# Attention's block rows as step sequences of their own, a third buffer for the high part of the split weights, one general temporary less

## The chip, the cores and the metric

One Trainium2 chip, one of its cores. The metric is the device time of one execution in microseconds (us); the median of several runs counts, and one more execution is profiled.

## The reference, cut to what matters

One layer: a normalized input, one projection into 57 column tiles of 128, three branches (RWKV-7 time mixing in six pairs of heads, causal pooling in four groups, stick-breaking attention in six pairs of heads), a gate on each, and an output projection. All in float32, 512 tokens of width 2048.

```python
h = _rms(x, norm_g[l])
proj = h @ w_in[l]
pa, pb, pc = _split(proj, (A_COLS, B_COLS, C_COLS))
...
y = jnp.concatenate([ya, yb, yc], axis=-1).astype(x.dtype) @ w_out[l]
x = x + y.astype(x.dtype)
```

The branch that the change rewrites is attention. Per block row of 128 queries:

```python
z = jnp.einsum('bhqd,bhkd->bhqk', q[:, :, q0:kend], k[:, :, :kend])
causal = jnp.arange(kend)[None, :] < (q0 + jnp.arange(SB_BLOCK))[:, None]
log_1m = jnp.where(causal, jax.nn.log_sigmoid(-z), 0.0)
after = lax.cumsum(log_1m, axis=3, reverse=True) - log_1m
w = jnp.where(causal, jnp.exp(jax.nn.log_sigmoid(z) + after), 0.0)
outs.append(jnp.einsum('bhqk,bhkd->bhqd', w, v[:, :, :kend]))
```

The cumulative sum over keys is what the kernel does with a scan on VectorE. RWKV's recurrence over tokens is done in eight chunks of 64 tokens, each a few matmuls that hand a state on to the next chunk.

## The kernel before

**The projection is the backbone.** Tiles are worked one after the other in the order of `tile_order`: for each pair p of heads q, k, v and gate of attention, then k, r of the next pair, v and gate of RWKV. A product in full precision is made of three matmuls in a reduced format (`three`): activations and weights are split into a high part and a low part, and high by high, low by high and high by low are summed (`hh`, `hl` for activations, `wh`, `wl` for weights). A column tile is 16 x 3 matmuls of 128x128 by 512 tokens, into a PSUM bank `pj` of which there are two.

**The weights come as a stream of halves**, 128x1024 each: 108 of the input projection and 32 of the output projection. For each, `split_weights` (L445) issues the load into `raw` on SyncE's queue (SP), casts it to `wh` on ScalarE and subtracts to `wl` on VectorE. `raw`, `wh` and `wl` have two buffers each. The next half is fetched when a half is begun, with a priority that puts it `AHEAD` = 300 in front of what the program has written so far.

**Everything else is side work**, written as Python generators (here: step sequences): `rwkv(p)`, `attention(p)`, `pooling(g)`. They advance in `pump`, called after every matmul of the projection. `Pace` keeps a model of when each engine is through with what, and a sequence yields a time: `need(...)` (tiles are ready and a PSUM bank is free, with a margin) or `soon(...)` (tiles ready, 1.5 us early allowed). `spawn` adds a sequence. The result is a fixed order on every engine; at run time each engine works its own list in order and waits by semaphores.

**Attention** makes the normalized q and k, splits them, and then does for each of the two heads three groups of block rows: widths 512, 512 (384 + 128) and 256. For each: matmuls into the bank `z`; ScalarE copies it to `w`; GpSimd masks the diagonal block (`affine_select`); ScalarE makes `n` (Abs, Exp, Ln) and `m` (Relu); one `soon(n, m)`; VectorE scans `n` and subtracts (`w<-w,n`); ScalarE takes the exponential (`w<-w`). The last three come out of one step. `n` has two buffers and `m` one. Then `w` is transposed (`wT`) and multiplied with v (`o`).

**RWKV** makes `bk`, `amr`, `bx` and the block inverses (`xblk`, `lt`), and at the end runs through the eight chunks: matmul `s`, then VectorE writes two pieces of `uv` (by `ec`), which the next chunk's `s` reads.

16 general temporaries of 128x528 (`TP`) are shared by all sequences. In the trace the ScalarE, VectorE and GpSimd work has the line L212 (a helper records it), matmuls L380, transposes L384, and DMAs L226.

Of the kernel before, what the change touches and what calls it, by code (L numbers as in the profile page):

```python
# [8 lines left out]
F32 = mybir.dt.float32  # L9
F32R = mybir.dt.float32r  # L10
AF = mybir.ActivationFunctionType
ALU = mybir.AluOpType

P = 128
# [43 lines left out]
DL = 4.0  # L58
QUICK = 1.8
SCAN = 150  # L60
TP = 16


def tile_order():
# [153 lines left out]
def hybrid_trunk_kernel(ctx: ExitStack, tc: tile.TileContext, x, xT, w_in, w_out, vecs, consts, up_w, pool_w, out):  # L218
    nc = tc.nc
# [20 lines left out]
    def name(s):  # L240
        uid[0] += 1
        return f"{s}_{uid[0]}"
# [6 lines left out]
    def tmp(s="t", cols=T):  # L249
        return tp.tile([P, TW], F32, tag="t", name=name(s))[:, 0:cols]  # L250
# [137 lines left out]
    def need(*tiles, tag=None, margin=MARGIN):  # L388
        def at():
            t = max([pace.ready.get(Pace.key(a), 0.0) for a in tiles] + [0.0])  # L390
            return margin + (max(t, pace.bank_at(tag, BANKS[tag])) if tag else t)

        return at
# [17 lines left out]
    def soon(*tiles):  # L411
        return need(*tiles, margin=-1.5)

    def spawn(gen):
        tasks.append([gen, lambda: 0.0])
# [27 lines left out]
    HK = KT // 2  # L443

    def split_weights(src):  # L445
        raw = wp.tile([P, HK * P], F32, tag="raw", bufs=2, name=name("raw"))
        dma(out=raw, in_=src)
        wh = wp.tile([P, HK * P], F32R, tag="wh", name=name("wh"))
        wl = wp.tile([P, HK * P], F32R, tag="wl", name=name("wl"))
        act.copy(out=wh, in_=raw)  # L450
        dve.tensor_tensor(wl, raw, wh.bitcast(F32), ALU.subtract)
        return wh, wl
# [101 lines left out]
    def rwkv(p):  # L554
# [8 lines left out]
        sq = tmp("sq")  # L563
# [54 lines left out]
        m1 = tmp("m1")  # L618
        bv = scratch(f"bv{p % 2}", "bv")
        dve.scalar_tensor_tensor(m1, rs, col(V_RK), kp, ALU.mult, ALU.mult)  # L620
        yield soon(rs)

# [171 lines left out]
        mu = gb("mu")  # L796
        block_sum(mu, bmean_r, yp2)
        dve.tensor_tensor(y, y, mu, ALU.subtract)
        sq = tmp("sq")
        act.activation(sq, y, AF.Square)  # L800
        sqp = split(sq)
# [2 lines left out]
        block_sum(var, bmean_r, sqp)  # L804
        act.activation(sq, var, AF.Ln, bias=eps_gn)
        act.activation(sq, sq, AF.Exp, scale=-0.5)
        dve.scalar_tensor_tensor(y, y, col(V_GNG), sq, ALU.mult, ALU.mult)
        dve.scalar_tensor_tensor(y, y, col(V_GNB), bv, ALU.add, ALU.add)
        gate = yt[Y_TILE[("a", p)]]
# [5 lines left out]
    def attention(p):  # L815
        while p > 0 and not done.get(("att", p - 1)):
            yield None
        qk = []
        for kind, gain, slot in (("cq", nvec[:, 12:13], "aq"), ("ck", vec[:, V_KN:V_KN + 1], "ak")):
            while (kind, p) not in got:  # L820
                yield None
            raw = got.pop((kind, p))
            dst = scratch(slot, kind)
            sq = tmp("qs")
            act.activation(sq, raw, AF.Square)
            sqp = split(sq)
            yield need(*sqp, tag="g")
            ms = gb("qm")
            block_sum(ms, bmean_r, sqp)
            y0, t = newton_rsqrt(ms, RMS_EPS, eps_rms, sq)  # L830
            dve.scalar_tensor_tensor(raw, raw, gain, y0, ALU.mult, ALU.mult)
            dve.tensor_tensor(dst, raw, t, ALU.mult)
            qk.append(dst)
        q, k = qk
        yield need(q, k)
        kr = tmpr("kr")
        act.copy(out=kr, in_=k)
        klo = tmpr("klo")
        dve.tensor_tensor(klo, k, kr.bitcast(F32), ALU.subtract)
        head = []  # L840
        for h in range(2):
            s = slice(h * HD, (h + 1) * HD)
            other = hi if h == 0 else lo
            q2 = ap.tile([P, T], F32R, tag="q2", name=name("q2"))
            k2 = ap.tile([P, T], F32R, tag="k2", name=name("k2"))
            act.copy(out=q2[s, :], in_=q[s, :])
            dve.tensor_tensor(q2[other, :], q[s, :], q2[s, :].bitcast(F32), ALU.subtract)
            act.copy(out=k2[s, :], in_=k[s, :])
            act.copy(out=k2[other, :], in_=k[s, :])
            kl2 = ap.tile([P, T], F32R, tag="kl2", name=name("kl2"))  # L850
            pool.tensor_copy(out=kl2[s, :], in_=klo[s, :])
            pool.tensor_copy(out=kl2[other, :], in_=klo[s, :])
            blocks = {}
            for segs, width in ((((3, 0),), 512), (((2, 0), (0, 384)), 512), (((1, 0),), 256)):
                yield need(q2, k2, kl2, tag="g")
                z = gb("z")
                for i, off in segs:
                    mm(z[:, off:off + (i + 1) * P], q2[:, i * P:(i + 1) * P], k2[:, 0:(i + 1) * P], True, False)
                    mm(z[:, off:off + (i + 1) * P], q2[:, i * P:(i + 1) * P], kl2[:, 0:(i + 1) * P], False, True)

                d0 = segs[0][0] * P
                nd = len(segs)
                pat = [[0, nd], [-1, P]] if nd > 1 else [[-1, P]]
                diag = lambda t: t[:, d0:d0 + nd * P].rearrange("p (a t) -> p a t", a=nd) if nd > 1 else t[:, d0:d0 + P]
                w = ap.tile([P, width], F32, tag=f"w{segs[0][0]}{h}", name=name("w"))
                act.copy(out=w, in_=z[:, 0:width])
                pool.affine_select(out=diag(w), in_=diag(w), pattern=pat, compare_op=ALU.is_gt, fill=-1e5, base=0, channel_multiplier=1)

                n = ap.tile([P, 512], F32, tag="n", bufs=2, name=name("n"))[:, 0:width]
                m = ap.tile([P, 512], F32, tag="m", bufs=1, name=name("m"))[:, 0:width]  # L870
                act.activation(n, w, AF.Abs)
                act.activation(n, n, AF.Exp, scale=-1.0)
                act.activation(n, n, AF.Ln, bias=1.0)
                act.activation(m, w, AF.Relu)
                yield soon(n, m)
                for i, off in segs:
                    sg = slice(off, off + (i + 1) * P)
                    dve.tensor_tensor_scan(n[:, sg][:, ::-1], n[:, sg][:, ::-1], m[:, sg][:, ::-1], 0.0, ALU.add, ALU.add)
                dve.tensor_tensor(w, w, n, ALU.subtract)
                act.activation(w, w, AF.Exp)  # L880
                for i, off in segs:
                    for j in range(i + 1):
                        blocks[(i, j)] = w[:, off + j * P:off + (j + 1) * P]
            head.append(blocks)
            if h == 0:
                while ("cv", p) not in got:
                    yield None
                vs = got.pop(("cv", p))
                yield need(vs, tag="g", margin=MARGIN + 2.0)
                vt = ap.tile([P, 4, P], F32, tag="vt", name=name("vt"))  # L890
                vps = gb("vps")
                for j in range(4):
                    transpose(vps[:, j * P:(j + 1) * P], vs[:, j * P:(j + 1) * P])
                act.copy(out=vt, in_=vps.rearrange("p (j c) -> p j c", j=4))

        o = None
        for js, width in (((0,), 512), ((1, 3), 512), ((2,), 256)):
            parts = []
            for h in range(2):
                yield need(*head[h].values(), tag="g", margin=MARGIN + 2.0)  # L900
                tps = gb("wT")
                pos = {}
                off = 0
                for j in js:
                    pos[j] = slice(off, off + T - j * P)
                    for i in range(j, 4):
                        transpose(tps[:, off:off + P], head[h][(i, j)])
                        off += P
                home = {(0, 0): "q2", (0, 1): "k2", (1, 0): "kl2", (2, 0): "q2", (2, 1): "k2"}.get((js[0], h))
                wt = ap.tile([P, T], F32, tag=home, name=name("wt"))[:, 0:width] if home else tmp("wt", width)  # L910
                act.copy(out=wt, in_=tps[:, 0:width])
                parts.append(wt)
            yield need(*parts, vt, tag="g" if o is None else None)
            if o is None:
                o = gb("o")
            for j in js:
                for h, s in ((0, lo), (1, hi)):
                    mm(o[s, j * P:T], vt[:, j, s], parts[h][:, pos[j]], j == 0, j == 2)
        while ("cg", p) not in got:
            yield None  # L920
        y = yt[Y_TILE[("c", p)]]
        dve.tensor_tensor(y, o, y, ALU.mult)
        put_away("c", p)
        done[("att", p)] = True
# [239 lines left out]
```

## Time and profile before

| | |
|---|---|
| runs | 1008.92, 1012.28, 1011.92 us; median 1011.92 |
| profiled execution | 1011.55 us, span 1009.8, mean granted clock 0.99 |
| TensorE (PE) busy | 983.2 us, 97% |
| VectorE (DVE) busy | 660.2 us, 65% |
| ScalarE (ACT) busy | 511.2 us, 51% |
| GpSimd (POOL) busy | 146.2 us, 14% |

The span runs from the first instruction to the last; 1.75 us of the profiled execution lie outside it. Matmuls overlap, so busy time on TensorE does not mean that it is at its peak. A wait is idle time of an engine just before an instruction, with the work whose end released it. The granted clock is a share of full speed. PEld is the loading of weights into TensorE, which overlaps the matmuls.

### The profile page before, as it was taken

What the parts mean: (1) busy time and instruction counts of PE and PEld (TensorE: products, weight loads), DVE (VectorE), ACT (ScalarE), POOL (GpSimd) and SP (SyncE); (2) the same over time, 40 slices, a digit from 0 to 9 for tenths busy, and PEclk for the clock granted to TensorE, in tenths of its full rate; (3) what the DMA queues carried; (4) which work ended last, traced back from release to release, by engine and by line L of the source; (5) the groups of instructions that cost most, each with busy time, mean ns of one, the idle gap of its engine ahead of it and who ended that gap; (6) DMA issues with size and microseconds to landing.
All of it is one profiled execution on the core that took longest, in us unless ns stands there. A gap on an engine that the chain in (4) does not pass through costs nothing.

```text
span 1009.8 us, 13791 instructions
## 1 busy us (share of the span) xinstructions
PE 983.2 (97%) x5132; PEld 790.0 (78%) x5132; DVE 660.2 (65%) x1249; ACT 511.2 (51%) x838; POOL 146.2 (14%) x204
## 2 busy tenths in 40 slices
PE   8989989999899999999999999999989999999998
PEld 7868877888678886788778887788867888888886
DVE  5269684878839786597957979387874666313222
ACT  5556654756546655657546565466652245211211
POOL 0031211122110302112111121202211010000000
PEclk9999999999999999999999999999999999999999
DMA  9621322132221323222231232312232248634241
GB/s 341 211 89 63 115 74 95 68 110 69 84 100 63 101 77 97 87 75 82 85 120 64 68 99 87 108 63 90 84 95 96 94 139 277 212 105 135 95 146 62
DMA packets 62211, 109.18 MB, mean 108 GB/s; under 512 B 29760, under 2 KB 31168, under 8 KB 62144
## 3 DMA queue, kind: packets, MB, share of 16 engines
q1 hardware_dynamic: 62144, 108.30, 32.0%
q8 instruction: 40, 0.66, 0.3%
q14 instruction: 27, 0.22, 0.1%
HBM read 98.84 MB, written 9.44 MB: 107 GB/s over the span
## 4 chain that ended last, share of the span: by engine, by line
PE 58%; DVE 24%; issue 9%; ACT 4%; POOL 3%; DMA 2%; SPq 0%; DVEq 0%; POOLq 0%
PE pj L380 30%; PE oacc L380 17%; DVE wl L212 4%; DVE xblk L212 3%; DVE pr L212 3%; DVE bx L212 3%; DVE u L212 2%; PE first L380 2%; DVE n L212 2%; PE gm L380 1%; DMA lt<-in_x 1%; PE o L380 1%; POOL e L212 1%; PE wT L384 1%; DVE bk L212 1%
## 5 line engine op out<-in xcount | busy, mean ns | idle before, releaser
L380 PE MATMUL pj<-hh,wl 128*128 128x512 f32 x864 | 345.1, 399 | 12.5 <-DVE wl L212 12.5
L380 PE MATMUL pj<-hh,wh 128*128 128x512 f32 x864 | 348.7, 404 | 2.3 <-ACT wh L212 2.0
L380 PE MATMUL pj<-hl,wh 128*128 128x512 f32 x864 | 344.8, 399 | 0.0
L212 DVE TENSOR_TENSOR wl<-raw,wh 128x1024 fp32r<-128x1024 f32 x140 | 175.3, 1252 | 173.5 <-ACT wh L212 173.1
L212 ACT CAST wh<-raw 128x1024 fp32r<-128x1024 f32 x140 | 146.4, 1046 | 198.7 <-PE oacc L380 115.9
L380 PEld LDWEIGHTS pj<-hh,wl 128*128 128x128 f32 x864 | 164.0, 190 | 49.9 <-DVE wl L212 16.4
L380 PEld LDWEIGHTS pj<-hh,wh 128*128 128x128 f32 x864 | 164.3, 190 | 38.1 <-ACT wh L212 4.0
L380 PEld LDWEIGHTS pj<-hl,wh 128*128 128x128 f32 x864 | 164.2, 190 | 32.9 <-issue 2.2
L380 PE MATMUL oacc<-wl,yh 128*128 128x512 f32 x256 | 100.0, 391 | 0.0
L380 PE MATMUL oacc<-wh,yl 128*128 128x512 f32 x256 | 99.6, 389 | 0.0
L380 PE MATMUL oacc<-wh,yh 128*128 128x512 f32 x256 | 99.6, 389 | 0.0
L212 POOL TENSOR_SCALAR e<-e 128x512 f32<-128x512 f32 x28 | 45.1, 1610 | 183.6 <-ACT e L212 179.0
L380 PEld LDWEIGHTS oacc<-wh,yl 128*128 128x128 f32 x256 | 48.1, 188 | 10.3 <-issue 0.2
L380 PEld LDWEIGHTS oacc<-wl,yh 128*128 128x128 f32 x256 | 48.1, 188 | 10.3 <-issue 0.2
L380 PEld LDWEIGHTS oacc<-wh,yh 128*128 128x128 f32 x256 | 48.1, 188 | 9.8
L212 DVE TENSOR_TENSOR u<-pj,rstd 128x512 f32<-128x512 f32 x50 | 34.4, 688 | 28.9 <-PE pj L380 27.9
L212 POOL TENSOR_TENSOR d<-u 128x512 f32<-128x512 f32 x25 | 30.8, 1231 | 145.9 <-DVE u L212 64.3
L212 ACT ACTIVATE e<-e 128x512 f32<-128x512 f32 x50 | 31.5, 630 | 36.1 <-POOL e L212 35.6
L212 DVE TENSOR_TENSOR xblk<-xblk,pr 128x60 f32<-128x60 f32 (+8 forms) x180 | 42.6, 236 | 5.1
L212 DVE TENSOR_TENSOR_SCAN n<-n,m 128x512 f32<-128x512 f32 (+3 forms) x48 | 40.4, 852 | 7.1 <-ACT n L212 7.1
L212 ACT ACTIVATE w<-w 128x512 f32<-128x512 f32 (+1 forms) x36 | 20.2, 560 | 48.4 <-DVE w L212 47.7
L212 DVE TENSOR_TENSOR pr<-xblk,nblk 128x60 f32<-128x60 f32 (+8 forms) x180 | 40.7, 226 | 5.1
(203 smaller groups left out, 1236.8 us busy)
## 6 DMA issues: line engine op xcount, KB each, us to landing
raw<-in_w_in SPq DMA_DIRECT2D x108, 512.0 KB, 3.4
raw<-in_w_out SPq DMA_DIRECT2D x32, 512.0 KB, 4.2
lt<-in_x SPq DMA_DIRECT2D x8, 512.0 KB
xr<-in_x SPq DMA_DIRECT2D x16, 256.0 KB, 5.5
out<-xr SPq DMA_DIRECT2D x16, 256.0 KB, 3.2
yin<-yd SPq DMA_DIRECT2D x14, 256.0 KB, 4.2
fr<-in_w_in SPq DMA_DIRECT2D x12, 256.0 KB, 7.1
nblk<-s SPq DMA_DIRECT2D x24, 128.0 KB, 4.0
```

Source lines behind the costliest of these rows:

```text
L212: return call(*args, **kw)
L380: pe.matmul(o, lhsT, rhs, start=start, stop=stop)
L384: pe.transpose(o, src, ident)
```

## The change

`wh` gets a third buffer. The work on one group of block rows after its mask becomes a function `weigh` that is spawned as a sequence of its own; at most two may be pending before their subtraction, and `m` gets a second buffer. Inside it a pause `soon(w)` stands ahead of Abs and another between subtraction and the last exponential, so that the exponential is issued in a later step. The transposes wait in Python until all ten blocks of a head are there. Some pauses are added in `rwkv` and in the normalization of q and k, and one general temporary is given up. The scratch for DMA descriptors is halved.

```diff
@@ -58,7 +58,7 @@
-TP = 16
+TP = 15
@@ -445,7 +445,7 @@
         raw = wp.tile([P, HK * P], F32, tag="raw", bufs=2, name=name("raw"))
         dma(out=raw, in_=src)
-        wh = wp.tile([P, HK * P], F32R, tag="wh", name=name("wh"))
+        wh = wp.tile([P, HK * P], F32R, tag="wh", bufs=3, name=name("wh"))
         wl = wp.tile([P, HK * P], F32R, tag="wl", name=name("wl"))
@@ -618,7 +618,7 @@
         dve.scalar_tensor_tensor(m1, rs, col(V_RK), kp, ALU.mult, ALU.mult)
-        yield soon(rs)
+        yield soon(m1)
@@ -796,6 +796,7 @@
         dve.tensor_tensor(y, y, mu, ALU.subtract)
+        yield soon(y)
         sq = tmp("sq")
@@ -804,6 +805,7 @@
         act.activation(sq, sq, AF.Exp, scale=-0.5)
+        yield soon(sq)
         dve.scalar_tensor_tensor(y, y, col(V_GNG), sq, ALU.mult, ALU.mult)
@@ -822,6 +824,7 @@
             sq = tmp("qs")
+            yield soon(raw)
             act.activation(sq, raw, AF.Square)
@@ -838,6 +841,7 @@
         head = []
+        pending = []
         for h in range(2):
@@ -865,22 +869,31 @@
                 w = ap.tile([P, width], F32, tag=f"w{segs[0][0]}{h}", name=name("w"))
                 act.copy(out=w, in_=z[:, 0:width])
                 pool.affine_select(out=diag(w), in_=diag(w), pattern=pat, compare_op=ALU.is_gt, fill=-1e5, base=0, channel_multiplier=1)
-
-                n = ap.tile([P, 512], F32, tag="n", bufs=2, name=name("n"))[:, 0:width]
-                m = ap.tile([P, 512], F32, tag="m", bufs=1, name=name("m"))[:, 0:width]
-                act.activation(n, w, AF.Abs)
-                act.activation(n, n, AF.Exp, scale=-1.0)
-                act.activation(n, n, AF.Ln, bias=1.0)
-                act.activation(m, w, AF.Relu)
-                yield soon(n, m)
-                for i, off in segs:
-                    sg = slice(off, off + (i + 1) * P)
-                    dve.tensor_tensor_scan(n[:, sg][:, ::-1], n[:, sg][:, ::-1], m[:, sg][:, ::-1], 0.0, ALU.add, ALU.add)
-                dve.tensor_tensor(w, w, n, ALU.subtract)
-                act.activation(w, w, AF.Exp)
-                for i, off in segs:
-                    for j in range(i + 1):
-                        blocks[(i, j)] = w[:, off + j * P:off + (j + 1) * P]
+                def weigh(w=w, segs=segs, width=width, blocks=blocks):
+
+                    n = ap.tile([P, 512], F32, tag="n", bufs=2, name=name("n"))[:, 0:width]
+                    m = ap.tile([P, 512], F32, tag="m", bufs=2, name=name("m"))[:, 0:width]
+                    yield soon(w)
+                    act.activation(n, w, AF.Abs)
+                    act.activation(n, n, AF.Exp, scale=-1.0)
+                    act.activation(n, n, AF.Ln, bias=1.0)
+                    act.activation(m, w, AF.Relu)
+                    yield soon(n, m)
+                    for i, off in segs:
+                        sg = slice(off, off + (i + 1) * P)
+                        dve.tensor_tensor_scan(n[:, sg][:, ::-1], n[:, sg][:, ::-1], m[:, sg][:, ::-1], 0.0, ALU.add, ALU.add)
+                    dve.tensor_tensor(w, w, n, ALU.subtract)
+                    pending.pop()
+                    yield soon(w)
+                    act.activation(w, w, AF.Exp)
+                    for i, off in segs:
+                        for j in range(i + 1):
+                            blocks[(i, j)] = w[:, off + j * P:off + (j + 1) * P]
+
+                while len(pending) > 1:
+                    yield None
+                pending.append(w)
+                spawn(weigh())
             head.append(blocks)
             if h == 0:
                 while ("cv", p) not in got:
@@ -897,6 +910,8 @@
         for js, width in (((0,), 512), ((1, 3), 512), ((2,), 256)):
             parts = []
             for h in range(2):
+                while len(head[h]) < 10:
+                    yield None
                 yield need(*head[h].values(), tag="g", margin=MARGIN + 2.0)
                 tps = gb("wT")
                 pos = {}
@@ -1152,7 +1167,7 @@
     from concourse.bass_utils import run_bass_kernel_spmd
 
     arrays = _pack(inputs)
-    nc = bacc.Bacc("TRN2", target_bir_lowering=False, num_devices=1, dynamic_dma_scratch_size=1024)
+    nc = bacc.Bacc("TRN2", target_bir_lowering=False, num_devices=1, dynamic_dma_scratch_size=512)
     args = {}
     for n, a in arrays.items():
         args[n] = nc.dram_tensor(f"in_{n}", a.shape, mybir.dt.from_np(a.dtype), kind="ExternalInput").ap()
```

How this moves instructions, at two places. First ScalarE in pair 1, the second head of attention, whose first row is `w_565`: `n` and `m` are the scan's inputs, `w_565<-w_565` is the last exponential, `wh` are casts of weights, `sq` and `yc` belong to RWKV's normalization, `wt` to the transposes. Before:

```order
L212 CAST wh_569_3460<-raw_568_3458 128x1024
L212 ACTIVATE n_566_3447<-n_566_3447 128x512
L212 ACTIVATE m_567_3448<-w_565_3442 128x512
L212 ACTIVATE n_566_3447<-n_566_3447 128x512
L212 ACTIVATE w_565_3442<-w_565_3442 128x512
L212 COPY w_572_3488<-z_571_3483 128x512
L212 ACTIVATE sq_555_3389<-var_575_3502,biases_91 128x512
L212 ACTIVATE n_573_3493<-w_572_3488 128x512
L212 CAST wh_580_3538<-raw_579_3536 128x1024
```

After, beginning three rows behind `m_569`, the last input of the scan of `w_565`:

```order
L212 ACTIVATE m_571_3428<-w_567_3419 128x512
L212 ACTIVATE n_570_3427<-n_570_3427 128x512
L212 ACTIVATE n_577_3487<-w_573_3440 128x256
L212 ACTIVATE n_570_3427<-n_570_3427 128x512
L212 ACTIVATE n_577_3487<-n_577_3487 128x256
L212 ACTIVATE m_578_3488<-w_573_3440 128x256
L212 ACTIVATE n_577_3487<-n_577_3487 128x256
L212 ACTIVATE sq_560_3386<-var_579_3496,biases_91 128x512
L212 COPY wt_581_3515<-wT_580_3510 128x512
L212 ACTIVATE sq_560_3386<-sq_560_3386 128x512
L212 ACTIVATE w_565_3408<-w_565_3408 128x512
L212 CAST wh_589_3583<-raw_588_3581 128x1024
```

The exponential of `w_565` stood two rows behind `m_567`, with a cast four rows later; now it stands thirteen rows behind `m_569`, with a cast (`wh_586`) one row behind `m_569` and the next just behind the exponential.

Second VectorE in pair 2, the first head, whose first row is `w_504`: `uv` is RWKV's state of a chunk, from the `s` matmul; `lt`, `amr` and `bx` from `gm` are masks of RWKV; the scans are the rows `n<-n,m`. Before:

```order
L212 TENSOR_TENSOR wl_514_3150<-raw_512_3147,wh_513_3149 128x1024
L212 TENSOR_TENSOR bx_482_2962<-gm_509_3119,kon_83 128x4x64
L212 SCALAR_TENSOR_TENSOR n_505_3102<-n_505_3102,m_506_3103 128x512
L212 TENSOR_TENSOR w_504_3097<-w_504_3097,n_505_3102 128x512
L212 TENSOR_SCALAR uv_476_2938<-s_516_3171,ec_254_1657 64x64 x2
L212 TENSOR_SCALAR uv_476_2938<-s_525_3213,ec_254_1657 64x64 x2
L212 TENSOR_TENSOR u_526_3220<-pj_496_3049,rstd_132 128x512
L212 TENSOR_TENSOR wl_531_3230<-raw_529_3227,wh_530_3229 128x1024
```

After, beginning one row behind the scan of `n_510`, the first row's:

```order
L212 TENSOR_TENSOR lt0_98<-gm_517_3160,kon_83 64x4x64
L212 TENSOR_TENSOR w_504_3098<-w_504_3098,n_510_3129 128x512
L212 TENSOR_SCALAR uv_476_2941<-s_521_3183,ec_259_1685 64x64 x2
L212 TENSOR_TENSOR amr_97<-gm_517_3160,kon_83 64x4x64
L212 TENSOR_TENSOR bx_492_3025<-gm_517_3160,kon_83 128x4x64
L212 TENSOR_TENSOR lt0_98<-gm_518_3161,kon_83 64x4x64
L212 TENSOR_TENSOR amr_97<-gm_518_3161,kon_83 64x4x64
L212 TENSOR_TENSOR bx_492_3025<-gm_518_3161,kon_83 128x4x64
L212 SCALAR_TENSOR_TENSOR n_512_3135<-n_512_3135,m_513_3136 128x384
L212 SCALAR_TENSOR_TENSOR n_512_3135<-n_512_3135,m_513_3136 128x128
L212 TENSOR_TENSOR q2_539_3277<-cq_435_2719,q2_539_3277 64x512
L212 TENSOR_SCALAR uv_476_2941<-s_526_3218,ec_259_1685 64x64 x2
```

The scans of the first and the second row have come together, and two writes of `uv` that stood in a row now have the masks and the second row's scan between them.

## Rows read from the trace of the kernel before

**Rows 1.** The page: busy time by engine, and the chain's shares by engine.

```profile
PE 983.2 (97%) x5132; PEld 790.0 (78%) x5132; DVE 660.2 (65%) x1249; ACT 511.2 (51%) x838; POOL 146.2 (14%) x204
...
PE 58%; DVE 24%; issue 9%; ACT 4%; POOL 3%; DMA 2%; SPq 0%; DVEq 0%; POOLq 0%
```

**Rows 2.** Waits: engine and operation, releaser, us in total, times, longest.

```profile
ACT w L212 <- DVE w L212: 47.7, 23, 3.8
...
PE pj L380 <- DVE wl L212: 12.5, 9, 2.4
...
PE pj L380 <- ACT wh L212: 2.0, 1, 2.0
...
PE s L380 <- DVE uv L212: 1.1, 3, 0.4
```

**Rows 3.** Windows: length, busy (instructions) PE, PEld, DVE, ACT, POOL, clock, DMA, GB/s.

```profile
265.10:268.50 3.40, 3.40 (x11) 2.73 (x11) 3.40 (x6) 1.85 (x5) 0.00 (x0) 0.50 0.40 154
503.00:506.40 3.40, 3.40 (x18) 2.86 (x17) 3.40 (x7) 1.89 (x4) 0.00 (x0) 1.00 0.39 146
739.50:742.90 3.40, 3.25 (x8) 2.57 (x9) 3.40 (x10) 2.79 (x8) 0.51 (x2) 0.50 0.44 159
```

**Rows 4.** Timeline of PE: start, length, operation, [idle before, releaser].

```profile
151.23 0.50 PE L380 MATMUL pj<-hh,wl 128*128 128x512 f32 x1 [1.57 <-DVE wl L212]
...
374.98 0.39 PE L380 MATMUL pj<-hh,wl 128*128 128x512 f32 x1
...
377.48 0.39 PE L380 MATMUL pj<-hh,wh 128*128 128x512 f32 x1
377.71 0.39 PE L380 MATMUL pj<-hl,wh 128*128 128x512 f32 x1
...
383.40 0.50 PE L380 MATMUL pj<-hh,wl 128*128 128x512 f32 x1 [1.85 <-DVE wl L212]
```

**Rows 5.** Timeline of ACT, same stretch.

```profile
377.54 0.63 ACT L212 ACTIVATE w<-w 128x512 f32<-128x512 f32 x1 [3.81 <-DVE w L212]
...
379.73 1.03 ACT L212 CAST wh<-raw 128x1024 fp32r<-128x1024 f32 x1
```

**Rows 6.** Timeline of DVE, same stretch.

```profile
373.95 1.22 DVE L212 TENSOR_TENSOR wl<-raw,wh 128x1024 fp32r<-128x1024 f32 x1
...
376.81 0.69 DVE L212 TENSOR_TENSOR w<-w,n 128x512 f32<-128x512 f32 x1
...
381.28 2.07 DVE L212 TENSOR_TENSOR wl<-raw,wh 128x1024 fp32r<-128x1024 f32 x1
```

**Rows 7.** Groups of DVE by form: count, busy us, mean ns, idle before, releasers.

```profile
L212 DVE TENSOR_TENSOR wl<-raw,wh 128x1024 fp32r<-128x1024 f32 x140 | 175.3, 1252 | 173.5 <-ACT wh L212 173.1
...
L212 DVE TENSOR_SCALAR uv<-s,ec 64x64 f32<-64x64 f32 x84 | 23.7, 282 | 15.7 <-PE s L380 14.8
...
L212 DVE TENSOR_TENSOR w<-w,n 128x512 f32<-128x512 f32 x24 | 16.8, 699 | 0.9
...
L212 DVE TENSOR_TENSOR_SCAN n<-n,m 128x512 f32<-128x512 f32 x12 | 14.6, 1217 | 4.9 <-ACT n L212 4.9
...
L212 DVE TENSOR_TENSOR lt<-gm,kon 64x256 f32<-64x256 f32 x24 | 10.1, 420 | 5.5 <-PE gm L380 5.1
```

**Rows 8.** Groups of ACT, same columns; +1 forms means mixed widths.

```profile
L212 ACT ACTIVATE n<-n 128x512 f32<-128x512 f32 (+1 forms) x72 | 39.7, 552 | 0.5
...
L212 ACT ACTIVATE w<-w 128x512 f32<-128x512 f32 (+1 forms) x36 | 20.2, 560 | 48.4 <-DVE w L212 47.7 <-DVE xblk L212 0.5
L212 ACT ACTIVATE n<-w 128x512 f32<-128x512 f32 (+1 forms) x36 | 20.1, 560 | 25.8 <-POOL w L212 24.7 <-POOL u L212 1.0
L212 ACT ACTIVATE m<-w 128x512 f32<-128x512 f32 (+1 forms) x36 | 19.7, 548 | 8.7 <-DVE n L212 8.7
```

**Rows 9.** The page's DMA issues: queue, count, KB each, us to landing.

```profile
raw<-in_w_in SPq DMA_DIRECT2D x108, 512.0 KB, 3.4
```

**Rows 10.** Timeline of POOL, same stretch as rows 5.

```profile
381.16 1.10 POOL L212 TENSOR_TENSOR d<-u 128x512 f32<-128x512 f32 x1 [2.00 <-issue]
```

## The prediction

> **What bounds the kernel now.** The page's busy table first: TensorE is busy for 983.2 of 1009.8 us, VectorE for 660.2, ScalarE for 511.2 [rows 1]. A change that takes nothing from TensorE's own work can only give back time in which TensorE stands still or runs slowly. The chain that ended last says where to look: beside TensorE's 58% it runs for 24% over VectorE, so TensorE waits here and there for something that VectorE makes [rows 1]. The waits name it: matmuls of the projection (`pj`) wait 12.5 us in nine places for `wl`, the low part of the split weights, and 2.0 us in one place for `wh`, the high part [rows 2]. TensorE's other waits are small and most of them belong to the start; `s` has 1.1 us in three places [rows 2]. That is 14.5 us of weight stalls.
>
> The stalls cost more than their length. After four of them (264.9, 383.4, 620 and 739.6 us) the granted clock is 0.50, the lower of its two levels (1.2 GHz); the first and the last stand in the table of windows with 11 and 8 matmul records, where the stretch at 503 us, after a stall too, shows 1.00 and 18 records [rows 3]. Each such stretch is 3.4 us at half speed, so it loses 1.7 us; four make 6.8. The weight stalls with their echo are worth 14.5 + 6.8 = **21.3 us**.
>
> Why does `wl` come late? The stall before 383.40 us, step by step. A half is 24 matmuls at 0.23 us (starts at 377.48 and 377.71 [rows 4]), 5.5 us. TensorE's last read of the old buffers is the matmul at 374.98 [rows 4], and two halves' buffers exist, so from 375.4 on the `wh` and `wl` that are needed at 381.1 could have been written. But ScalarE, which takes its work in order, stands until 377.54 before `w<-w`, attention's last exponential, with 3.81 us of idle time [rows 5]. It waits for VectorE's `w<-w,n`, which starts at 376.81 behind the scan [rows 6]. Behind this exponential stand three more operations, and only then, at 379.73, the cast `wh` [rows 5]. `wl` follows at 381.28, is 2.07 us long in place of its mean of 1.25 [rows 6, 7], and TensorE stands from 381.5 to 383.4. Over the whole run ScalarE idles 47.7 us before such exponentials and 24.7 us before `n<-w`, which waits for GpSimd's mask [rows 8]; VectorE's `wl` waits 173.1 us for `wh` [rows 7]. An idle ScalarE costs nothing; that a cast stands behind the waiting row does.
>
> **The change, part by part.**
>
> *The exponential leaves the head of ScalarE's queue.* The number of instructions is the same: 36 each of `n<-w`, `m<-w` and the last `w<-w`, 72 of `n<-n` [rows 8]. In the order of after, the exponential stands seven rows (pair 2) to thirteen rows (pair 1, the fence) behind the last of the scan's inputs, before it stood right behind. Scan and subtraction take 1.22 + 0.70 us for a 512-wide row [rows 7]; seven rows of 0.55 us are 3.9, thirteen 7.2, so they pass under other ScalarE work, and casts stand ahead of the exponential. I take the 47.7 us as mostly gone from where casts are queued.
>
> *The third `wh` buffer.* The cast can run one half earlier, 5.5 us, if its raw weights are there. The raw buffers are still two, and raw comes free with the `wl` that reads it; a load takes 3.4 us [rows 9]. With `wl` early in its half the cast gains most of 5.5 us; with `wl` as late as at 373.95 [rows 6] the raw data land at about 375.2 + 3.4 = 378.6 for a half needed at 386.4, a lead of 7.8 where before it was at best 5.7. So 2 to 5 us more room on a cast whose stalls were 2.4 us at longest [rows 2]. `wl` keeps two buffers and 5.5 us of room, of which it needs 1.25; freed from ScalarE, it depends on VectorE's queue alone. At its fullest that queue has by the order, with the means of its rows, 9.4 and 6.5 us of work in two halves that follow one another (5.5 each) and is early enough by some 0.5 us, so I leave 1 of the 12.5 us standing.
>
> *The clock.* Without these stalls the four slow stretches go: 6.8 us.
>
> *What is added.* Three rows of a head are now issued close together, and their scans reach VectorE's queue one behind the other, ahead of `uv`, on which the chain of `s` matmuls waits (chunk by chunk the state of RWKV). Take pair 2, the place of the fence on VectorE. From the copy `w_504<-z` to `m_511` ScalarE has four rows of 0.55 us (`n`, `n`, `n`, `m`), a cast of 1.03 [rows 5, 8] and five copies; two of these I take at 0.5 and three, half as wide or less, at 0.35 (estimates below `w<-w`'s 0.56 [rows 8]): 5.3 us. VectorE adds scan 1.22, `lt` 0.42, `w` 0.70 and two `uv` at 0.28: 2.9 [rows 7]. That is 8.2 us, and GpSimd's mask adds a few tenths. TensorE has in the same time 26 large matmuls (5.9 us) and small ones that by their columns are worth 2 us: 7.9. So the `s` that needs this `uv` waits 0.6 or so. The next `uv` stands behind five mask operations (2.1 us), two scans (1.5, an estimate from the 512-wide one's 1.22) and `q2` (0.7, as `w`), in all 4.9 with itself, against 13 large matmuls and some transposes, 3.5 to 3.9 us: about 1.0. In all 1.6 us a pair. Four pairs (1 to 4) have the two chains side by side: **6.4 us**, where before it was 1.1. None of these waits is over 1.5 us, and after such a one (151.23, 1.57 us [rows 4]) no slow stretch stands, so I add no clock.
>
> *Edits at nothing.* The added points at which a sequence pauses (`sq`, `y`, `raw`, `m1`) move rows by a few places; their releasers are ready then. Temporaries 16 to 15: a temporary that is missing would stall its writer on ScalarE or VectorE, under the 35 to 49% that these stand idle [rows 1]; bounds 0 to 2 us. The start chain shifts by two matmuls and one weight cast: between -1 and +1. `m` with two buffers takes away `m`'s wait of 8.7 us [rows 8], which is ScalarE's and on no path. SP's queue: `s2`'s store now stands behind two more loads of raw weights, each of which waits for its `wl`; by the order it is issued no later than its data are ready. TensorE's own work is unchanged.
>
> The sum against the profiled execution, 1011.55 us, which is 0.4 under the median of 1011.92: 1011.55 - 14.5 - 6.8 = 990.3 with nothing added; + 1 for what is left of `wl`; + 6.4 for `s`: 997.7. **Forecast 998 us.** Its own range is 994 to 1003: `s` at half or at almost twice its price.
>
> **The rivals.**
>
> *R1, part of the stalls is merely moved.* The `s` waits are 2 us at eight places (16 us in all) since ScalarE reaches the first row's inputs later than the means say: a second cast in front is 1.03 us, and `n<-w` waited 24.7 us for GpSimd's mask [rows 8], which stays. Against it: VectorE stands ready for `s` before `uv`, 14.8 us in all [rows 7], so its queue has some slack there. 990.3 + 16 = 1006; with two or three slow stretches on top 1010, which is no change.
>
> *R2, `wl` stays late.* Two `wl` buffers, and VectorE, not ScalarE, was the reason: the `wl` at 381.28 took 2.07 us beside GpSimd's `d`, 1.10 us at 381.16 [rows 6, 10], 0.82 over the mean, and it is TensorE's wait of 1.85 almost by half. The mean of 1.25 over 140 says that such collisions are rare [rows 7]: 140 x (1.25 - 1.22) = 4 us in all, 1.22 being the `wl` at 373.95 [rows 6]. Against R2 also: at 383.4 `wh` was 4.4 us late, the collision 0.8. If half of the 12.5 stays, with two slow stretches: 990.3 + 6.3 + 3.4 + 6.4 = 1006. The Trainium skill ("SBUF — State Buffer", section "SBUF: two separate sides") says that a VectorE operation with two SBUF inputs and a GpSimd operation share a port pair as an exclusive lock, held for a whole instruction, the other blocking fully. By that rule a `wl` that starts in a GpSimd operation of 1.1 us is late by as much whatever its buffers, which speaks against the change; the row of 2.07 us agrees with it.
>
> *R3, slower.* The same eight places as in R1, but with the scans' wait for ScalarE in full: the exponential's 3.8 us [rows 5] turn up on `uv` instead. Gain and loss meet at 21.3 / 8 = 2.7 us a place. Above that each wait is also long enough for a slow stretch of 1.7. At 3 us: 990.3 + 8 x 4.7 = 1028. Against it: the twelve 512-wide scans waited only 4.9 us for ScalarE in all [rows 7].
>
> *R4, it does nothing.* The raw weights' two buffers keep the casts where they are, and another row of ScalarE takes the exponential's place as the one that waits: 1009 to 1014. Against it: the casts stand by the order one half earlier, and the wait of 3.81 us had no other reason than that its input was made just before.
>
> **How the numbers follow.** Forecast (994 to 1003) 0.57; all stalls gone and `s` free (988 to 994) 0.12; R1 or R2 in part (1003 to 1008.9) 0.12; R4 or R1 with its stretches (1008.9 to 1015) 0.10; R3 (over 1015) 0.09. A measurement tells 0.3%, 3 us, from no change. Faster is thus 0.57 + 0.12 + 0.12 = 0.81, same 0.10, slower 0.09. The range of 988 to 1009 holds 0.81.
>
> **What would show it.** Right: `pj <- wl` under 3 us and `pj <- wh` at nothing in the waits of after; the granted clock at 1.00 from 80 us to the end; ScalarE's wait before `w<-w` well under 20 us; `s <- uv` grown to between 3 and 10 us in places of about 1 us. Wrong: `s <- uv` above 16 us or slow stretches behind it (R1, R3); `pj <- wl` still above 6 (R2); `w<-w` still 40 us (R4).

## The result, and the profile after

The changed kernel takes **1023.29 us** (median of 4 runs, 1019.83 to 1024.63) against 1011.96 (4 runs): ratio 1.0114, interval 1.0101 to 1.0127. It is 11.3 us slower, where 998 was forecast and 988 to 1009 was the range.

The profiled execution took 1024.2 us, its span is 1022.4, 12.6 more than before. Three terms make that up. TensorE's busy time rises from 983.2 [rows 1] to 987.1, so its idle time (span less busy) rises from 26.6 to 35.3 us: **8.7**. The granted clock stands at half in seven stretches of 3.4 us, before in six and in the last 0.6 us of the span; at 1.7 us for a stretch that is **1.4** more. The remaining 2.5 are work of TensorE that takes longer at full clock, in a pair of matmuls, below.

The page of after, and the larger of TensorE's waits (columns as in rows 2):

```profile
PE 987.1 (97%) x5132; PEld 792.6 (78%) x5132; DVE 660.7 (65%) x1249; ACT 509.3 (50%) x838; POOL 146.5 (14%) x204
```

```profile
PE o L380 <- ACT wt L212: 6.4, 4, 2.1
PE pj L380 <- DVE wl L212: 4.5, 4, 1.3
PE s L380 <- DVE uv L212: 3.4, 4, 1.3
PE qm L380 <- DVE sl L212: 3.0, 2, 2.8
PE rb L373 <- DVE dg L212: 2.8, 1, 2.8
PE gm L380 <- issue: 1.9, 1, 1.9
...
PE gm L380 <- ACT vt L212: 1.5, 1, 1.5
PE y L380 <- DVE uv L212: 1.3, 1, 1.3
```

(`issue`: the profile shows nothing that was waited for.) The waits that the change was aimed at did shrink: `wl` from 12.5 to 4.5, `wh` from 2.0 to none [rows 2]. In their place stand waits for side work of several kinds, each once to four times. The largest is new: `o`, attention's product with v, waits 6.4 us in four places for the copy `wt`.

ScalarE's own waits say what came instead:

```profile
ACT wh L212 <- DMA raw<-in_w_in: 59.4, 21, 7.4
...
ACT wh L212 <- DMA raw<-in_w_out: 23.3, 7, 5.4
ACT w L212 <- DVE w L212: 19.5, 14, 3.0
```

The wait before the last exponential fell from 47.7 [rows 2] to 19.5, as forecast. But casts now wait 82.7 us for their raw weights, a wait that the kernel before doesn't have among its rows. One of the four places where `o` waits, in pair 1, on four engines (timelines; SPq is SyncE's DMA queue):

```profile
280.95 1.22 DVE L212 TENSOR_TENSOR wl<-raw,wh 128x1024 fp32r<-128x1024 f32 x1
```

```profile
278.77 0.54 SPq L226 DMA_DIRECT2D s<-xblk  x1
281.06 1.88 SPq L226 DMA_DIRECT2D yd<-y  x1
284.90 1.32 SPq L226 DMA_DIRECT2D lt<-s  x3
286.33 0.38 SPq L226 DMA_DIRECT2D raw<-in_w_in  x1
```

```profile
287.26 1.30 ACT L212 ACTIVATE e<-e 128x512 f32<-128x512 f32 x2 [1.85 <-POOL e L212]
291.15 1.04 ACT L212 CAST wh<-raw 128x1024 fp32r<-128x1024 f32 x1 [2.59 <-DMA raw<-in_w_in]
292.11 0.58 ACT L212 COPY wt<-wT 128x512 f32<-128x512 f32 x1
```

```profile
285.46 0.60 PE L384 MATMUL wT<-kon,w 128*128 128x128 f32 x4
...
289.64 1.07 PE L380 MATMUL o<-wt,vt 128*64 128x512 f32 x2
292.74 1.53 PE L380 MATMUL o<-wt,vt 128*64 128x512 f32 x2 [2.02 <-ACT wt L212]
```

Read from the bottom. `o` of the second head waits until 292.74 for `wt`, whose transposes were done at 286.1. ScalarE did nothing from 288.6 to 291.15: it stood at the cast, with `wt` behind it. The cast waited for a raw load that was issued at 286.33 and landed 4.8 us later. The load's buffer had been free since 282.2, when `wl` at 280.95 ended, but SyncE works its list in order too, was at `yd<-y` until 282.9 and then stood at `lt<-s`, RWKV's reload of the block inverses, which waits for the store `s<-xblk` to land. Ahead of the cast, the gate's exponentials `e<-e` wait 1.85 us for GpSimd; they too stand before `wt` now. In the kernel before, at the same place, `wt` waits only for its transposes, and `e` comes after it:

```profile
272.47 1.03 ACT L212 CAST wh<-raw 128x1024 fp32r<-128x1024 f32 x1
274.49 0.59 ACT L212 COPY wt<-wT 128x512 f32<-128x512 f32 x1 [0.99 <-PE wT L384]
275.90 0.63 ACT L212 ACTIVATE e<-d 128x512 f32<-128x512 f32 x1 [0.82 <-DVE d L212]
```

```profile
278.05 1.08 PE L380 MATMUL o<-wt,vt 128*64 128x512 f32 x4
```

This row also shows the 2.5 us. Before, the four records of the two heads' first `o` run side by side, on two halves of TensorE's columns, in 1.08 us. After, the first head's two take 1.07 alone and the second's 1.07 or more behind them; that is so in four pairs, before in one. Three times 1.07 is 3.2, somewhat more than is to be explained.

The other three places of `o` are not all like this one. At 169.34 (0.73 us) a cast that waited 7.4 us for its load stands further ahead in ScalarE's list. At 413.25 and 742.71 (1.55 and 2.12 us) no cast waits for a load in the 8 us ahead of `wt`; it stands behind the gate's exponentials, and with every load early (raw3, below) these two waits stay:

```profile
740.52 0.63 ACT L212 ACTIVATE e<-e 128x512 f32<-128x512 f32 x1 [0.88 <-POOL e L212]
...
742.10 0.56 ACT L212 COPY wt<-wT 128x512 f32<-128x512 f32 x1
```

```profile
742.71 1.07 PE L380 MATMUL o<-wt,vt 128*64 128x512 f32 x2 [2.12 <-ACT wt L212]
```

So 2.8 of the 6.4 us of `o` have a late raw load behind them, and 3.7 the place that the split gave to `wt`.

The lower clock (windows, columns as in rows 3):

```profile
54.40:57.60 3.20, 2.70 (x4) 1.50 (x5) 1.03 (x4) 0.00 (x0) 0.00 (x0) 0.50 0.03 8
57.70:61.00 3.30, 3.30 (x9) 2.57 (x8) 1.87 (x4) 1.00 (x1) 2.16 (x4) 0.50 0.00 0
...
293.30:296.50 3.20, 3.20 (x11) 2.01 (x10) 1.53 (x4) 0.92 (x2) 0.00 (x0) 0.50 0.56 191
...
743.90:747.10 3.20, 3.20 (x10) 2.61 (x11) 2.86 (x11) 0.44 (x1) 0.00 (x0) 0.50 0.38 145
```

The four stretches behind weight stalls [rows 3] are gone; others stand behind the new waits: two in a row behind `rb`, two behind `o` (the last two rows here), one behind `qm` at 208, one behind `gm` at 477.6. The remaining one, at the very start, is in both kernels.

### The profile page after: what moved, and what is told of

Read it like the earlier page. It is cut to its first block, busy times and chain, and to the rows that moved or that the text cites. A ratio compares the mean times of both kernels' runs of the same rounds, so it can differ in the third digit from the quotient of the medians.

```text
span 1022.4 us, 13871 instructions
## 1 busy us (share of the span) xinstructions
PE 987.1 (97%) x5132; PEld 792.6 (78%) x5132; DVE 660.7 (65%) x1249; ACT 509.3 (50%) x838; POOL 146.5 (14%) x204
## 4 chain that ended last, share of the span: by engine, by line
PE 43%; DVE 6%; issue 3%; ACT 3%; POOL 1%; DMA 1%; POOLq 0%; SPq 0%; DVEq 0%; ACTq 0%
PE pj L380 21%; PE oacc L380 16%; DVE wl L212 1%; POOL e L212 1%; PE o L380 1%; DVE bx L212 1%; ACT e L212 1%; ACT n L212 1%; PE wT L384 1%; PE gh L380 1%; DMA xblk<-s 1%; DVE n L212 0%; PE y L380 0%; DVE u L212 0%; DMA yin<-yd 0%
## 5 line engine op out<-in xcount | busy, mean ns | idle before, releaser
L380 PE MATMUL pj<-hh,wh 128*128 128x512 f32 x864 | 345.1, 399 | 0.1
L380 PEld LDWEIGHTS oacc<-wl,yh 128*128 128x128 f32 x256 | 48.1, 188 | 10.1 <-issue 0.2
L212 DVE TENSOR_TENSOR pr<-xblk,nblk 128x60 f32<-128x60 f32 (+8 forms) x180 | 43.7, 243 | 4.9
L212 ACT ACTIVATE n<-n 128x512 f32<-128x512 f32 (+1 forms) x72 | 39.4, 554 | 0.1
```

The lines of the kernel that those rows point to most:

```text
L212: return call(*args, **kw)
L380: pe.matmul(o, lhsT, rhs, start=start, stop=stop)
```

## The experiments

Every kernel was timed beside the kernel before on the same chip. Since each run's mean granted clock is known, its time can be parted: clock loss (span times the missing share) and the rest, which is the time at full clock. The granted clock is on record to three places, so one run's clock loss is known to 0.5 us. Medians of runs, so the parts need not add up to the time; ratios with their interval; the profiled execution of a kernel is one of these runs and can lie at the edge of them. A kernel's order is a plan made ahead, and an edit can change all of it: of ScalarE's 838 instructions, 790 (split_only) and 808 (raw3) stand in the same order as in the changed kernel, but only some 540 to 570 in o_margin, no_exp_pause and no_small. What these three cost or give back can't be laid to the edited line alone.

| kernel | us | ratio to before | clock loss | rest |
|---|---|---|---|---|
| before | 1011.6 | | 10.1 | 1002 |
| changed | 1023.3 | 1.0114 (1.0101 to 1.0127) | 12.8 | 1011.5 |
| wh3 | 1009.8 | 0.9990 (0.9976 to 1.0005) | 3.5 | 1006.4 |
| split_only | 1012.6 | 1.0011 (0.9995 to 1.0026) | 8.1 | 1004.5 |
| raw3 | 1013.3 | 1.0017 (1.0006 to 1.0027) | 5.1 | 1007.2 |
| o_margin | 1014.7 | 1.0038 (1.0025 to 1.0052) | 6.1 | 1008.7 |
| before_raw3 | **1002.9** | 0.9925 (0.9907 to 0.9943) | 3.0 | 999.9 |
| no_exp_pause | 1015.2 | 1.0038 (1.0013 to 1.0062) | 5.6 | 1010.7 |
| no_small | 1024.7 | 1.0133 (1.0116 to 1.0150) | 10.2 | 1014.5 |
| raw3_no_exp_pause | 1009.5 | 0.9982 (0.9972 to 0.9991) | 5.0 | 1004.4 |
| raw_only | 1010.9 | 0.9983 (0.9971 to 0.9996) | 6.0 | 1003.7 |
| all3 | 1030.8 | 1.0176 (1.0130 to 1.0222) | 18.0 | 1013.1 |

**wh3**, the third buffer alone, in the kernel before.

```diff
-TP = 16
+TP = 15
-        wh = wp.tile([P, HK * P], F32R, tag="wh", name=name("wh"))
+        wh = wp.tile([P, HK * P], F32R, tag="wh", bufs=3, name=name("wh"))
```

> The kernel before with the third buffer for wh and one temporary less, attention as it was. Two theories of the 11 us that the change costs. A (early casts): with three wh buffers a cast stands in ScalarE's queue one half earlier, ahead of its raw weights, which still have two buffers; ScalarE stands at the cast and all behind it is late. B (split): the split step sequences let the transposes' copy wt slip behind the exponentials of the next gate, so that the o matmuls wait for it. A expects here 1012 to 1020 us, with ScalarE's wh waiting 60 us or more for the raw loads. B expects 995 to 1004: wl waits under 4 us, and no wait of o for wt above 0.5.

Neither: 1009.8 us, no difference that can be told. The casts do wait for raw loads, as A has it, 78 us:

```profile
ACT wh L212 <- DMA raw<-in_w_in: 46.2, 19, 4.3
...
ACT wh L212 <- DMA raw<-in_w_out: 31.9, 7, 6.0
```

```profile
PE pj L380 <- DVE wl L212: 7.4, 7, 1.8
PE o L380 <- ACT wt L212: 4.6, 4, 1.7
PE wT L384 <- ACT w L212: 3.4, 4, 0.9
```

Weight stalls go from 14.5 to 7.4 us, and 8 us of `o` and `wT` come. At full clock the kernel is 4.4 us slower; the waits are shorter (1.8 at most), the clock loss falls by 6.6 us, and the two nearly cancel.

**split_only**, the changed kernel with two `wh` buffers.

```diff
-        wh = wp.tile([P, HK * P], F32R, tag="wh", bufs=3, name=name("wh"))
+        wh = wp.tile([P, HK * P], F32R, tag="wh", name=name("wh"))
```

> The changed kernel with two wh buffers again: attention's step sequences, the pauses and the 15 temporaries stay. A expects 1000 to 1009 us, o waiting under 2 us for wt and wh waiting little for raw loads. B expects 1015 to 1024, with o waiting 5 to 7 us for wt in three or four places, as in the changed kernel (6.4 in four).

1012.6, between the two; `o` waits 2.7 us in two places, the last two of the four, and no cast waits for a raw load.

```profile
PE o L380 <- ACT wt L212: 2.7, 2, 2.1
```

So neither part costs the 11 us by itself: they cost it together. TensorE's order is nearly that of the changed kernel (5122 of 5132 matmuls and transposes); what moves is mainly the casts, one half earlier on ScalarE, and on VectorE the `wl`. That is worth 10.7 us here, where in the unsplit kernel it was worth -2, within the noise.

**raw3**, the changed kernel with a third buffer for the raw weights.

```diff
-TP = 15
+TP = 13
-        raw = wp.tile([P, HK * P], F32, tag="raw", bufs=2, name=name("raw"))
+        raw = wp.tile([P, HK * P], F32, tag="raw", bufs=3, name=name("raw"))
```

> The changed kernel with a third buffer for the raw weights too, paid with two temporaries (13). A expects ScalarE's waits of wh for raw loads to fall from 82.7 us (59.4 and 23.3) to under 25, and 1003 to 1013 us. B expects them to fall likewise, but o still waits 5 us or more for wt, and 1018 to 1024.

1013.3, just above A's upper end and far from B: 10 us back, in nearly the same order on every engine. Casts wait 1.7 us for raw loads in place of 82.7. `o` still waits 3.8 us, in the two places where no load was late.

```profile
ACT wh L212 <- DMA raw<-in_w_in: 1.7, 3, 1.2
```

```profile
PE o L380 <- ACT wt L212: 3.8, 2, 2.3
```

In the two profiles TensorE's idle time falls by 3.7 us and the stretches at half clock from seven to three, worth 6.8 us. Not all of that hangs on a wait that went: `o` at 732.82 still waits 2.27 us, and no slow stretch follows, where one followed the 2.12 us at 742.71 in the changed kernel.

**o_margin**, the changed kernel with the `o` matmuls planned 2 us later.

```diff
-            yield need(*parts, vt, tag="g" if o is None else None)
+            yield need(*parts, vt, tag="g" if o is None else None, margin=MARGIN + 2.0)
```

> The changed kernel with the o matmuls planned 2 us later (margin 4.5 in place of 2.5 on the need for wt). If the o waits are what the change costs, 6.4 us of waits go, 3.4 us in which the two heads' first o matmuls ran one after the other and not side by side, and two stretches of half clock behind them (3.4): 1023 - 13 = 1010. If the loss sits elsewhere (start, qm, gm, s), 1016 to 1022, with other waits in their place.

1014.7, between the 1010 and the 1016 to 1022. `o` waits no more, but `wl` does, for 14.7 us in 13 places:

```profile
PE pj L380 <- DVE wl L212: 14.7, 13, 3.8
```

At full clock 2.8 us came back, of the clock loss 6.7. 8.6 of the 13 us that were put on the late `wt` came back, and other waits stand in its place. As the whole order moved with the margin, the price of the late `wt` alone stays open.

**before_raw3**, the kernel before with three `wh` and three raw buffers (TP 13).

> The kernel before with three buffers for wh and for raw (13 temporaries); attention unsplit. Theory A in a sharper form (A2): the early casts cost because ScalarE stands at them for raw loads (78 us with wh alone made three), so that o waits 4.6 us for wt and wT 3.4 us for w. With the loads early these 8 us go: 1000 to 1005 us, wh waiting under 10 us for raw. Rival C: the early casts cost nothing of weight and the time is the two programs' other waits: 1008 to 1012 as with three wh buffers alone (1009.8).

1002.9: within A2's range, **faster than both kernels**, by 0.75% (0.57 to 0.93) than the one before. The casts' waits for raw loads are gone, and of the weight stalls and `o` this is left:

```profile
PE pj L380 <- DVE wl L212: 7.9, 8, 1.8
PE wT L384 <- ACT w L212: 3.5, 4, 0.9
...
PE o L380 <- ACT wt L212: 1.7, 1, 1.7
```

```profile
ACT w L212 <- DVE w L212: 37.6, 30, 4.0
...
ACT wh L212 <- DMA raw<-in_w_in: 0.3, 1, 0.3
```

The exponential still waits 37.6 us at the head of ScalarE's queue. It costs little now, because the cast that stood behind it stands ahead: behind the wait that ends at 374.05 (3.0 us) now stands the cast of the next half, at 376.24, whose first matmul is at 383.93. Against wh3 only the third raw buffer and two temporaries differ, and the order hardly: with the loads early, 6.9 us go. Three temporaries fewer do no harm that shows.

**no_exp_pause**, the changed kernel without the pause that let the exponential go later.

```diff
                     pending.pop()
-                    yield soon(w)
                     act.activation(w, w, AF.Exp)
```

> The changed kernel without the pause between subtraction and last exponential: block rows are still sequences of their own. Theory B2: that pause is what delays attention so far that the second copy wt falls behind the exponentials of the next gate; in this program's order wt stands just behind two casts. B2 expects o's waits to fall from 6.4 to under 3 us and w<-w's wait for VectorE to rise from 19.5 back to 35 or more: 1010 to 1016. A2 alone expects the casts before wt to hold it all the same: o 4 us or more and 1018 to 1024.

1015.2, in B2's range: `o` waits 1.4 us, and 8 us come back, nearly all of it clock loss (12.8 to 5.6). The wait of `w<-w` rose only to 24.9, not to 35. The casts wait even longer for raw loads, 117 us, in a faster kernel: the sum of these waits is no measure of what they cost. That it depends on what stands behind them is likely, but not shown.

```profile
ACT wh L212 <- DMA raw<-in_w_in: 100.5, 28, 7.6
...
ACT w L212 <- DVE w L212: 24.9, 18, 3.7
ACT wh L212 <- DMA raw<-in_w_out: 16.7, 4, 5.0
```

**no_small**, the changed kernel without the pauses on `sq`, `y`, `raw` and with `rs` for `m1`.

> The changed kernel without the four small pauses (y, sq, raw, and m1 in place of rs). The prediction costed them at nothing. If that holds, 1020 to 1026 us with o still waiting 5 us or more. If they carry a part of the loss (qm's 3.0 us, var's 1.0, gm's 3.9), 1012 to 1018 and these waits gone.

1024.7, no gain, so these edits don't carry the loss. But `o` has no wait left in the list, where 5 us or more were expected, and others (`wl` 11.1, `q` 11) wait more; the casts wait 89 us for raw loads, much as in the changed kernel. The loss doesn't need the waits of `o`: with the order, other places wait, and the sum stays.

**raw3_no_exp_pause**, both cures.

> Both cures in the changed kernel: three raw buffers (13 temporaries) and no pause before the last exponential. If A2 and B2 hold side by side, o waits under 2 us, wh under 10 us for raw: 1002 to 1008 us. If the split sequences themselves cost (s, y, qm, dec waits of VectorE's and ScalarE's queues), 1009 to 1014, about the 1013.3 of three raw buffers alone.

1009.5, in the second range, though `o` waits no more and the casts wait under 10 us: the split costs too. Against no_exp_pause only the raw buffers and two temporaries differ, and the order hardly (831 of ScalarE's 838): 5.8 us go with the casts' waits for loads, 117 us there and 7 here.

```profile
ACT wh L212 <- DMA raw<-in_w_in: 6.9, 3, 3.5
```

With the same three raw and three `wh` buffers the unsplit kernel takes 1002.9, so what is left of the change (block rows as sequences of their own, the small pauses, the second `m`, the halved scratch) still costs 6 to 7 us, spread over waits of at most 2.5 us each (`wl` 9.8, `gh` 2.9, `dec` 2.5, `gm` 2.0). What each of these hangs on was not taken apart and stays open, and so does the halved scratch, which was not timed alone.

**raw_only**, the kernel before with three raw buffers, `wh` two (TP 14).

> The kernel before with a third buffer for the raw weights alone (14 temporaries), wh still two. If the gain of three raw and three wh buffers (1002.9 us) is a joint one, casts here still wait for their buffer and stand behind the last exponential: 1010 to 1013 us with wl waits of 10 us or more. If earlier loads alone are what helps, 1003 to 1006.

1010.9: the gain of `before_raw3` is a joint one. `wl`'s wait is 12.4 us and `wh`'s 2.0, as before. So a third raw buffer gives 10.0, 6.9 and 5.8 us where `wh` has three buffers (raw3, before_raw3, raw3_no_exp_pause), and 1 us where it has two.

**all3**, the kernel before with three buffers for raw, `wh` and `wl` (TP 12).

> The kernel before with three buffers for raw, wh and wl (12 temporaries). With raw and wh alone 7.9 us of wl waits were left in eight places. If these are waits for wl's own buffer, they go under 3 us: 995 to 1000. If VectorE's queue makes wl late whatever its buffers, 1001 to 1006.

Outside both: `wl` waits no more at all, and the kernel takes 1030.8.

```profile
PE wT L384 <- ACT w L212: 13.6, 8, 2.6
PE qm L380 <- DVE sl L212: 10.5, 6, 2.1
```

VectorE works without a gap ahead of most of these waits, so it is the order that makes them, not a missing buffer. In five of the six waits of `qm`, four `bx` of RWKV (0.7 us each) stand shortly ahead of the split `sl`, where in before_raw3 they do not; in the four longest waits of `wT` the subtraction `w<-w,n` stands behind a `wl`. A temporary fewer goes with the third `wl` buffer, so the buffer's own part is not shown. The profiled run is the fastest of the four by 9 us, with a clock loss of 8.6 where the median is 18.0.

## Why the prediction was wrong, point by point

*What bounds the kernel.* Right: weight stalls with their echo in the clock. `before_raw3` ends part of them and gets 8 us, 7 of which are clock loss. wh3 loses 6.6 us less to the clock, where 6.8 was put on the four stretches; that the numbers meet is luck in part, for one stretch behind a weight stall stays there, and the one at 70.5, at the start, goes.

*The exponential.* Right in its size: 47.7 us of ScalarE's wait fell to 19.5, `n<-w`'s for GpSimd from 24.7 [rows 8] to 5.1. Wrong in what it is worth: before_raw3 has 37.6 us of the wait left and is the fastest.

*The third `wh` buffer.* **This step failed.** It asked how much room the cast gains, put it at 2 to 5 us, and had no term for what an early cast does to the queue that it stands in. It saw that the raw buffers are two and a load takes 3.4 us, and made of it a limit on the gain (and rival R4, "it does nothing"). It didn't ask what stands behind a cast that is early in ScalarE's queue and has no data. A cast queued before its load holds the queue: 82.7 us of waits in ScalarE, and behind it, in two of the four places, the copy `wt`. That raw3 gives 10 of the 11 us back in the same order, and two buffers of `wh` give 10.7 (split_only), shows that the early casts without data cost this; by which of TensorE's waits the other microseconds pass was not followed place by place. It is 10 of the 25 us between forecast and result. The sentence on SyncE's queue looked the wrong way round: it asked whether `s2`'s store is late behind raw loads; at 286.33 it is the raw load that comes 4 us late, behind `lt<-s`.

*What is added on `s`.* Near: 6.4 us were expected, 3.4 on `s` and 1.3 on `y` for the same `uv` were measured, at most 1.3 in one place and with no slow stretch behind those at 340.9 and 367.4, as said.

```profile
340.93 0.46 PE L380 MATMUL s<-uv,bx 128*128 128x128 f32 x2 [1.29 <-DVE uv L212]
```

But it was the only new wait in the sum. The order was read at the two places that the stalls had pointed to; for ScalarE's copies `wt`, moved behind the next gate's exponentials in the same order, no term was made: 3.7 us of `o` in the two places that stay in raw3. This list failed too: with the loads early, raw3 still takes 15 us more than the forecast, and its waits of `o` (3.8), `qm` (3.3), `dec` (2.5) and `gm` (2.0) stand in no term of the sum.

*The clock.* 6.8 us of gain became 1.4 of loss. The forecast took the old stretches away and put none behind new waits, on the ground that these were under 1.5 us. `o` waits 2.0 and 2.1 us where a stretch follows, and the ground itself does not hold: at 476.7 `gm` waits 1.5 us, 2 us after a wait of 0.5, and a stretch follows.

*The start.* Between -1 and +1 was expected. `rb` waits 2.8 in place of 1.2 us, and two stretches at half clock follow where one stood at 70.5: about 3.3 us.

*Weight stalls.* 1 us was to be left; 4.5 are. The temporary at nothing: two fewer do no harm that shows, in nearly the same order (raw_only). The small pauses at nothing: nothing speaks against it (no_small), but the order there is another one.

*The rivals.* R2: `wl` was left with 4.5 us, and its mean length went only from 1.25 [rows 7] to 1.24, so collisions with GpSimd are not what made the kernel slower. R3 had the right sign, but by another place: it put 3 us on `uv`. R4 named the raw buffers, and took them for harmless. No rival had a wait of the weight stream that holds other work.

## What to carry to other kernels

On engines that work in order, a buffer more for one link of a chain doesn't just give slack: it lets that link be queued earlier, ahead of its own inputs, and then everything behind it waits. Give the link before it the same depth (here worth 6 to 10 us), and before pricing the gain list what is queued behind the moved instruction and who waits for that. Two edits that cost nothing each can cost 1% together, so time them apart and together.

## What the runs showed that was not expected

The clock loss of one kernel varies from run to run: wh3's mean granted clock lies between 0.993 and 1.000 in ten runs, 0 to 7 us. So one profile's slow stretches say little about a median. Parting the clock loss off helps where it varies most (no_exp_pause: the runs spread over 7.8 us, the time at full clock over 3.7), but not everywhere: in before_raw3 the runs spread over 1.1 us and the time at full clock over 3.1. And a third `wl` buffer, with one temporary fewer and no weight stall left at all, made the kernel 1.8% slower.
